# A two-layer mixer on one core: the first modulation vectors computed in quarters instead of halves, the tokens loaded in the same column pieces

## The chip, the cores and the metric

The program runs on one core of a Trainium2 chip. The metric is the device time of one execution in microseconds, and lower is better. Three runs of the kernel before are at hand; their median stands below, beside one profiled execution with its trace.

## What is computed

A two-layer transformer-like mixer works on 512 latent tokens (`x`, four tiles of 128 rows) and 256 context tokens (`ctx`, two tiles), each a vector of 1024 columns, all in float32. Each layer begins with a modulation: two conditioning vectors, one for `x` and one for `ctx`, are multiplied with `w_mod` and give six vectors of 1024 columns; the first two of them, a shift and a scale, turn the tokens into the input `h` of the in-projection:

```
mod = silu_c @ w_mod[l] + b_mod[l]
sh1, sc1, g1, sh2, sc2, g2 = [m[:, None, :] for m in jnp.split(mod, 6, axis=-1)]
...
h = x * (1.0 + sc1) + sh1
h_c = x_ctx * (1.0 + sc1c) + sh1c
proj = h @ w_in[l]
proj_c = h_c @ w_in[l]
```

The columns of `proj` go to attention, a gated MLP, pooling and a Fourier mix; an out-projection, a layer norm and a SwiGLU network with a second layer norm follow. Everything behind `proj` is the same in both kernels, apart from where a few instructions of layer 0's end stand.

## The kernel before

**Products.** Each float32 operand is split into two halves of a shorter format, the rounded value and the rest: ScalarE (ACT) casts, VectorE (DVE) subtracts (`split`, L167 to L170), and each product is three matmuls on TensorE (PE) into one accumulator (`mm3`, L172 to L175). The weights go the same way: `wload` loads a block of 832 or 1024 columns into a staging buffer, ACT casts it and DVE subtracts. There are four staging buffers and five buffers for split weights, so a cast of a new block waits until the matmuls of the block that had its buffer are through.

**Order.** The program is written as plain Python loops with generators that are advanced a step at a time (`filler`, `fill`), and a scheduler then sets the order of the instructions on each engine; an engine takes its instructions strictly in that order. Nearly all loads are issued by one queue (SP) in order. In the built program each load signals on one of eight semaphores, taken in turn, and waits for the load that had the semaphore before it to land; at the start bias loads issued by ACT hold four of the eight, and four loads of `w_mod` are in flight.

**The start.** `mods(0, (0, 1), c0, n, early=True)` computes the two vectors that layer 0's in-projection needs, for 2n columns: eight loads of `w_mod`, one per block k of 128 rows, then four small matmuls per k (L285), a bias add, transposes into columns (L312) and two copies per vector into `modT` (L315 to L319). Before the change it is called twice, for columns 0 to 511 (`ma`) and 512 to 1023 (`mb`), each with loads of 512 KB. The queue brings, in this order: `ma`'s eight loads, the first halves of four token tiles (256 KB each), the first two blocks of `w_in` (416 KB each; A0 and A2, for k = 0, 1 and k = 2, 3), the first halves of the two ctx tiles, `mb`'s eight loads, the second halves of all six tiles, then the blocks A4 and A6 of `w_in`, then blocks B1, B2 and so on (512 KB each), which the next stage multiplies with.

**The in-projection.** `inproj` goes over k = 0 to 7. For each k, `make_h` transposes the block of the six tiles on PE (L379: four for `x`, two for `ctx`), ACT applies scale and shift out of `modT` (L381), ACT casts and DVE subtracts (`u` tiles), and 18 matmuls follow: twelve for `x` into double banks (`pd`), six for `ctx` into `ps`. Blocks k = 0 to 3 need `modT` of the first half, 4 to 7 of the second. Behind `make_h` the loop advances `filler`, which holds `mb`, by two steps while k < 4 (a step is one k of `mb`). The splits of the weight blocks A4, A6, B1, B2, B3 and B4 stand on ACT and DVE between the splits of the tokens. Behind k = 7 comes the stage of the B blocks.

## Time and profile before

| | |
|---|---|
| device time, median of three runs | 1658.34 us (1655.94 to 1658.73) |
| device time of the profiled execution | 1661.08 us |
| its span, first to last instruction | 1659.3 us |
| mean granted TensorE clock | 0.984 |
| PE busy | 1573.3 us, 95% of the span |
| DVE busy | 1049.8 us, 63% |
| ACT busy | 764.9 us, 46% |
| DMA, mean over the span | 146 GB/s |

The profiled execution takes 1.78 us more than its span, and stands 2.74 us above the median. PE is busy for 95% of the span; the table alone does not tell where the rest lies, nor what the engines wait for there. The chain of work that ended last has 81% of the span on PE, 6% on DVE, 5% on DMA and 4% on ACT.

### The profile page before, as it was taken

The page shows a single profiled execution, that of the slowest core. Times are in us where ns is not written, and L with a number is a line of the kernel's source. Part 1 is how long each engine was busy: PE and PEld are TensorE (multiplying, and loading weights), DVE is VectorE, ACT ScalarE, POOL GpSimd, SP SyncE. Part 2 cuts the span into 40 slices and gives each one's busy share as a digit, 9 for nine tenths or more (in the row PEclk, how much of TensorE's full clock was granted, in tenths as well). Part 3 has the DMA queues.
Part 4 walks back from the last instruction along what each step waited for, and adds up shares of the span by engine and source line. Part 5 has one row for each costly group of instructions (what it writes and reads, how often), then busy time and mean ns, then how long its engine had stood idle before and what let it go on. Part 6 is the DMA issues. An engine that isn't in the chain of part 4 may idle for free.

```text
span 1659.3 us, 23905 instructions
## 1 busy us (share of the span) xinstructions
PE 1573.3 (95%) x9129; PEld 1361.8 (82%) x9129; DVE 1049.8 (63%) x1619; ACT 764.9 (46%) x1381; POOL 221.4 (13%) x308
## 2 busy tenths in 40 slices
PE   7998989999999999999999988989999999998997
PEld 4885668988899999997677774759988999997785
DVE  1445476876675665654457674557867888885676
ACT  2523455783653443443324543247865544553221
POOL 0232011341000000002001032422320000001003
PEclk9999999999999999999999999999999999999998
DMA  9325624118522332346965636560047344455551
GB/s 348 104 63 193 211 88 129 50 52 271 157 83 70 106 105 88 120 127 214 369 190 162 184 119 251 168 190 26 26 136 220 109 127 125 126 161 178 176 157 51
DMA packets 180503, 241.81 MB, mean 146 GB/s; under 512 B 10874, under 2 KB 127468, under 8 KB 180388
## 3 DMA queue, kind: packets, MB, share of 16 engines
q1 hardware_dynamic: 180356, 240.26, 45.3%
q8 instruction: 72, 1.18, 0.3%
q14 instruction: 43, 0.35, 0.1%
q10 hardware_dynamic: 32, 0.02, 0.0%
HBM read 215.30 MB, written 24.94 MB: 145 GB/s over the span
## 4 chain that ended last, share of the span: by engine, by line
PE 81%; DVE 6%; DMA 5%; ACT 4%; issue 2%; POOL 1%; SPq 1%; POOLq 0%; DVEq 0%; ACTq 0%
PE pd L1204 23%; PE pd L173 10%; PE pd L174 9%; PE pd L175 9%; PE ps L173 5%; PE ps L174 5%; PE ps L175 5%; PE ps L1204 4%; PE ps L747 3%; PE ps L731 2%; PE ps L285 2%; DVE w L169 2%; PE pd L285 2%; DMA u<-in_w_mod_dram 1%; ACT w L168 1%
## 5 line engine op out<-in xcount | busy, mean ns | idle before, releaser
L169 DVE TENSOR_TENSOR w<-s,w 128x1024 fp32r<-128x1024 f32 (+2 forms) x285 | 350.5, 1236 | 199.5 <-ACT w L168 198.0
L168 ACT CAST w<-s 128x1024 fp32r<-128x1024 f32 (+2 forms) x285 | 292.6, 1030 | 320.8 <-PE pd L1204 111.7
L1204 PE MATMUL pd<-u,w 128*128 128x256 f32 (+1 forms) x1938 | 297.2, 306 | 4.9 <-DVE w L169 3.1
L1204 PEld LDWEIGHTS pd<-u,w 128*128 128x128 f32 x1938 | 280.4, 189 | 10.6 <-ACT f L1258 4.5
L173 PE MATMUL pd<-w,u 128*128 128x512 f32 (+5 forms) x728 | 277.0, 381 | 7.0 <-ACT u L471 3.0
L174 PE MATMUL pd<-w,u 128*128 128x512 f32 (+5 forms) x728 | 274.3, 377 | 1.0 <-DVE w L169 1.0
L175 PE MATMUL pd<-w,u 128*128 128x512 f32 (+5 forms) x728 | 272.1, 375 | 0.0
L173 PEld LDWEIGHTS pd<-w,u 128*128 128x128 f32 x728 | 139.6, 192 | 50.4 <-issue 13.4
L174 PEld LDWEIGHTS pd<-w,u 128*128 128x128 f32 x728 | 140.0, 192 | 33.5 <-issue 10.1
L175 PEld LDWEIGHTS pd<-w,u 128*128 128x128 f32 x728 | 139.9, 192 | 29.9 <-issue 6.7
L168 ACT CAST u<-y 128x512 fp32r<-128x512 f32 (+3 forms) x186 | 94.9, 530 | 149.2 <-PE ps L175 102.8
L169 POOL TENSOR_TENSOR u<-y,u 128x512 fp32r<-128x512 f32 (+1 forms) x60 | 79.4, 1331 | 245.3 <-ACT u L168 223.9
L169 DVE TENSOR_TENSOR u<-y,u 128x512 fp32r<-128x512 f32 (+3 forms) x126 | 67.0, 551 | 70.9 <-ACT u L168 64.6
L174 PE MATMUL ps<-u,w 128*128 128x256 f32 (+2 forms) x288 | 93.0, 325 | 0.1
L175 PE MATMUL ps<-u,w 128*128 128x256 f32 (+2 forms) x288 | 92.7, 324 | 0.0
L173 PE MATMUL ps<-u,w 128*128 128x256 f32 (+2 forms) x288 | 91.9, 327 | 0.6 <-ACT f L1131 0.3
L169 DVE TENSOR_TENSOR u<-ps,u 128x512 fp32r<-128x512 f32 (+2 forms) x106 | 67.0, 655 | 35.8 <-ACT u L168 34.8
L173 PE MATMUL ps<-w,u 128*128 128x512 f32 (+1 forms) x208 | 81.2, 397 | 4.6 <-DVE u L169 4.6
L174 PE MATMUL ps<-w,u 128*128 128x512 f32 (+1 forms) x208 | 81.9, 394 | 3.5 <-DVE w L169 3.5
L175 PE MATMUL ps<-w,u 128*128 128x512 f32 (+1 forms) x208 | 81.6, 392 | 0.0
L168 ACT CAST u<-ps 128x512 fp32r<-128x512 f32 (+2 forms) x106 | 56.9, 563 | 39.3 <-PE ps L835 19.4
L1204 PE MATMUL ps<-u,w 128*128 128x384 f32 (+1 forms) x456 | 73.4, 310 | 0.0
(255 smaller groups left out, 2541.6 us busy)
## 6 DMA issues: line engine op xcount, KB each, us to landing
s<-in_w_ffn_dram SPq DMA_DIRECT2D x154, 512.0 KB
s<-in_w_out_dram SPq DMA_DIRECT2D x50, 512.0 KB
s<-in_w_mod_dram SPq DMA_DIRECT2D x48, 512.0 KB
u<-in_w_mod_dram SPq DMA_DIRECT2D x32, 512.0 KB
s<-in_w_in_dram SPq DMA_DIRECT2D x16, 512.0 KB
f<-in_w_mod_dram SPq DMA_DIRECT2D x16, 512.0 KB
yd<-f SPq DMA_DIRECT2D x19, 384.0 KB
y<-yd SPq DMA_DIRECT2D x88, 64.0 KB
```

The source lines that it names most:

```text
L168: c = A_.copy(out=hi, in_=src)
L169: (eng or V_).tensor_tensor(out=lo, in0=src, in1=f(hi), op=ALU.subtract)
L173: T_.matmul(ps, lhsT=ll, rhs=rh, start=start, stop=False)
L174: T_.matmul(ps, lhsT=lh, rhs=rl, start=False, stop=False)
L175: return T_.matmul(ps, lhsT=lh, rhs=rh, start=False, stop=stop)
L285: T_.matmul(ps[32 * j:32 * j + 32, :n], lhsT=sst[:, k, :], rhs=ws[j // 2][:, (j % 2) * n:(j % 2 + 1) * n], start=(k == 0), stop=(k == KD - ...
L731: T_.transpose(pt[:, o:o + P], es[t2][:, k * P:(k + 1) * P], ident)
L747: T_.matmul(av[:, 0:256], lhsT=vt[k][:, h, :], rhs=pts[k // 2][:, a, (k % 2) * 256:(k % 2 + 1) * 256], start=(k == 0 and a == 1), stop=(k ...
L1204: T_.matmul(ps, lhsT=A[u][:, k], rhs=B[k][:, v], start=first and k == 0 and i == 0, stop=last and k == 3 and i == 2, skip_group_check=True)
```

## The change

The first half of the modulation is computed in two quarters: `ma` for columns 0 to 255 and `mc` for 256 to 511, each with n = 128 and eight loads of 256 KB; `mb`, the second half, stays as it was. The tokens come in pieces of the same columns: 256, 256 and 512. The queue's order is now: `ma`, six token pieces of 128 KB, A0, `mc`, six pieces of 128 KB, A2, `mb`, six pieces of 256 KB, A4, A6, B1. Up to A4 it is the same bytes: 8.4 MB of `w_mod`, 3.1 MB of tokens, 0.85 MB of `w_in`, in 16 + 12 + 2 loads before and 24 + 18 + 2 after. There are twelve small bias loads on ACT's queue instead of eight. `filler` holds `mc` and `mb`; the loop advances it by five steps for k = 0 and 1 and four for k = 2 and 3, and empties `mc` ahead of k = 2. `modT` for blocks 0 and 1 now comes from `ma`, for 2 and 3 from `mc`. Two further edits touch the end of layer 0: `split` returns both its instructions, and the first part of layer 1's `make_h` (`hook`) is to be issued behind the last split of `feat`. The list `pe` and the buffers `xr_` are not read by anything.

```diff
--- before.py
+++ after.py
@@ -166,13 +166,15 @@
 
     def split(hi, lo, src, eng=None):
         c = A_.copy(out=hi, in_=src)
-        (eng or V_).tensor_tensor(out=lo, in0=src, in1=f(hi), op=ALU.subtract)
-        return c
+        return c, (eng or V_).tensor_tensor(out=lo, in0=src, in1=f(hi), op=ALU.subtract)
 
     def mm3(ps, lh, ll, rh, rl, start, stop):
         T_.matmul(ps, lhsT=ll, rhs=rh, start=start, stop=False)
         T_.matmul(ps, lhsT=lh, rhs=rl, start=False, stop=False)
-        return T_.matmul(ps, lhsT=lh, rhs=rh, start=False, stop=stop)
+        pe[0] = T_.matmul(ps, lhsT=lh, rhs=rh, start=False, stop=stop)
+        return pe[0]
+
+    pe = [None]
 
     def behind(ins, earlier):
 
@@ -210,12 +212,13 @@
     sst = cp.tile([P, KD, 32], F32, name="sst")
     gd = drp.tile([2, 2, 2, D], F32, name="gd")
     xn = drp.tile([LX, D], F32, name="xn")
+    xr_ = [drp.tile([P, D], F32, name=f"xr{i}") for i in range(NTX)]
     xc = drp.tile([LC, D], F32, name="xc")
     rd = [[drp.tile([P, D], F32, name=f"rd{l}_{i}") for i in range(NT)] for l in range(2)]
     yd = [[drp.tile([P, LJ], F32, name=f"yd{l}_{i}") for i in range(NF)] for l in range(2)]
 
 
-    bte = [cp.tile([P, 256], F32, name=f"bte{i}") for i in range(2)]
+    bte = [cp.tile([P, n], F32, name=f"bte{n}_{i}") for i, n in enumerate((256, 128, 128))]
     cr = Y(P)
     nc.sync.dma_start(out=cr[0:8], in_=g["c"].rearrange("o (k p) -> (o k) p", p=P))
     nc.sync.dma_start(out=cr[8:16], in_=g["c_ctx"].rearrange("(k p) -> k p", p=P))
@@ -449,9 +452,11 @@
                     w = getw(("A", l, gi, k), 1)
                 if l == 0:
                     extras(k)
+                    while len(filler) > 1 and k == 2:
+                        fill(1)
                 make_h(k, grp)
                 if l == 0 and k < 4:
-                    fill(2)
+                    fill(5 if k < 2 else 4)
                 if l and gi and len(filler) > 1:
                     fill(1)
                 for (st, t), a in zip(grp, acc):
@@ -1207,6 +1212,7 @@
         passes = [[(X, t) for t in range(4)]] if final else [[(C, 0), (C, 1), (X, 0)], [(X, 1), (X, 2), (X, 3)]]
 
         done = {}
+        cut = [None, None]
 
         def feat(pi, ft):
 
@@ -1230,7 +1236,8 @@
             d = U(F32R, 2 * n).rearrange("p (a b) -> p a b", a=2)
             c = split(d[:, 0], d[:, 1], y)
             if (pi, ft - 3) in done:
-                behind(c, done[(pi, ft - 3)])
+                behind(c[0], done[(pi, ft - 3)])
+            cut[:] = c
             return d, w2
 
         def unit(ft, w):
@@ -1324,7 +1331,8 @@
                     if len(filler) > 2 and (pi or ft > 1):
                         fill(1)
                     if pi and 5 <= ft < 5 + KD:
-                        hook(res, ft - 5)
+                        with tc.issue_after(cut[0].ins), tc.issue_after(cut[1].ins):
+                            hook(res, ft - 5)
                 if ft >= 8 and ft % 2 == 0 and len(ya) < len(tiles):
                     st, t = tiles[len(ya)]
                     y = FT()
@@ -1382,21 +1390,25 @@
     phase("inp")
     toks = {(st.s, t): I(n=D) for st, t in allg}
 
-    def xload(hf, grp):
+    def xload(c0, c1, grp):
         for st, t in grp:
-            nc.sync.dma_start(out=toks[(st.s, t)][:, hf * 512:(hf + 1) * 512],
-                              in_=g["x" if st.s == 0 else "ctx"][0, t * P:(t + 1) * P, hf * 512:(hf + 1) * 512])
-
-    ma = mods(0, (0, 1), 0, 256, early=True)
+            nc.sync.dma_start(out=toks[(st.s, t)][:, c0:c1],
+                              in_=g["x" if st.s == 0 else "ctx"][0, t * P:(t + 1) * P, c0:c1])
+
+    ma = mods(0, (0, 1), 0, 128, early=True)
     next(ma)
-    xload(0, allg[:4])
+    xload(0, 256, allg)
+    ahead(1)
+    mc = mods(0, (0, 1), 256, 128, early=True)
+    next(mc)
+    xload(256, 512, allg)
     ahead(2)
     mb = mods(0, (0, 1), 512, 256, early=True)
-    xload(0, allg[4:])
     next(mb)
-    xload(1, allg)
+    xload(512, 1024, allg)
     run(ma)
-    filler.append(mb)
+    filler.extend([mc, mb])
+
     one = lambda: PD()[:, 0]
     later = [mods(0, (2, 3), 0, 512, bank=one), mods(0, (4, 5), 0, 512, bank=one)]
     pars = [params(0), params(1)]
```

The scheduler gives the changed program another order. On PE, at the end of the transposes of k = 0 and the first product of the in-projection, the kernel before has (`i` are token tiles, `ps` and `pd` accumulators, `w_19` the block A0, `u_287` the split `h` of `x`):

```order
L379 MATMUL ps_288<-ident,i_171 128x128
L379 MATMUL ps_288<-ident,i_172 128x128
L379 MATMUL ps_298<-ident,i_173 128x128
L379 MATMUL ps_298<-ident,i_174 128x128
L173 MATMUL pd_283<-w_19_201,u_287 128x416
L174 MATMUL pd_283<-w_19_201,u_287 128x416
L175 MATMUL pd_283<-w_19_201,u_287 128x416
```

In the changed kernel the same place on PE reads (`u_217` to `u_231` are the eight loads of `mc`, `sst` the conditioning vectors, and `u_318` the split `h`):

```order
L382 MATMUL ps_329<-ident,i_178 128x128
L382 MATMUL ps_329<-ident,i_179 128x128
L288 MATMUL ps_336<-u_217,sst 32x128 x4
L288 MATMUL ps_336<-u_219,sst 32x128 x4
L288 MATMUL ps_336<-u_221,sst 32x128 x4
L288 MATMUL ps_336<-u_223,sst 32x128 x4
L288 MATMUL ps_336<-u_225,sst 32x128 x4
L288 MATMUL ps_336<-u_227,sst 32x128 x4
L288 MATMUL ps_336<-u_229,sst 32x128 x4
L288 MATMUL ps_336<-u_231,sst 32x128 x4
L172 MATMUL pd_314<-w_19_208,u_318 128x416
```

The 32 matmuls of the second quarter, eight rows of four, now stand between the last transposes of k = 0 and the first product. Of the 32 matmuls of `mb` (rows like the eight, with 256 columns), 24 stand ahead of the first product of k = 1 before and the last eight ahead of that of k = 2; after, sixteen stand ahead of each. All of `mb` is ahead of k = 2's products in both kernels.

On ACT, from the activation of k = 2 to the split of k = 3, the kernel before has (`y` are activated tokens with 512 columns for `x` and 256 for `ctx`; `w_52`, `w_65`, `w_80`, `w_98` are the casts of A4, A6, B1 and B2):

```order
L381 ACTIVATE y_394<-ps_391,modT 128x256
L168 CAST u_390<-y_394 128x256
L381 ACTIVATE y_430<-ps_425,modT 128x512
L168 CAST w_52_376<-s_51_375 128x832
L168 CAST u_424<-y_430 128x512
L168 CAST w_65_468<-s_64_467 128x832
L381 ACTIVATE y_437<-ps_434,modT 128x256
L168 CAST w_80_553<-s_79_552 128x1024
L168 CAST u_390<-y_437 128x256
L168 CAST w_98_660<-s_97_659 128x1024
```

The changed kernel has, from the activation of k = 2 for `x` on (`w_63`, `w_78`, `w_91` are the casts of A4, A6 and B1; `u_454` is the split of `ctx`, `u_496` that of `x` for k = 3):

```order
L384 ACTIVATE y_450<-ps_445,modT 128x512
L168 CAST u_444<-y_450 128x512
L384 ACTIVATE y_458<-ps_455,modT 128x256
L168 CAST w_63_440<-s_62_439 128x832
L168 CAST u_454<-y_458 128x256
L168 CAST w_78_549<-s_77_548 128x832
L384 ACTIVATE y_502<-ps_497,modT 128x512
L168 CAST w_91_625<-s_90_624 128x1024
L168 CAST u_496<-y_502 128x512
L384 ACTIVATE y_509<-ps_506,modT 128x256
L168 CAST u_454<-y_509 128x256
```

The cast of A4 stood behind both splits of k = 2, ahead of the split of `x` for k = 3; now it stands one split earlier, ahead of the `ctx` split of k = 2, and the casts of A6 and B1 stand ahead of the `x` split of k = 3. DVE's rows of the same splits moved alike.

Further on ACT, around k = 4 in the kernel before, the cast of B3 (`w_116`) stands so:

```order
L381 ACTIVATE y_487<-ps_482,modT 128x512
L381 ACTIVATE y_495<-ps_492,modT 128x256
L168 CAST w_116_771<-s_115_770 128x1024
L168 CAST u_481<-y_487 128x512
L168 CAST u_491<-y_495 128x256
```

In the changed kernel the cast of B3 stands behind both splits of k = 4, and the cast of B4 (`w_129`) stands as follows around k = 6:

```order
L384 ACTIVATE y_657<-ps_652,modT 128x512
L384 ACTIVATE y_665<-ps_662,modT 128x256
L168 CAST w_129_884<-s_128_883 128x1024
L168 CAST u_651<-y_657 128x512
L168 CAST u_661<-y_665 128x256
```

A cast of a weight block that waits for its buffer thus stands ahead of the two token splits of k = 4 before, and of k = 6 after. Behind that the rows of all engines are in the same order until the end of layer 0, where six small DVE operations (L368 to L370) move back by some 55 us of the program and, at the start of layer 1's in-projection, four PE instructions stand earlier.

## Rows read from the trace of the kernel before

**Rows 1.** The page: busy time of PE, and the span.

```profile
span 1659.3 us, 23905 instructions
...
PE 1573.3 (95%) x9129; PEld 1361.8 (82%) x9129; DVE 1049.8 (63%) x1619; ACT 764.9 (46%) x1381; POOL 221.4 (13%) x308
```

**Rows 2.** Stretches: length; PE, PEld, DVE, ACT, POOL busy; PEclk; DMA share; GB/s.

```profile
10.00:20.00 10.00, 7.23 (x50) 2.15 (x46) 0.79 (x5) 0.00 (x0) 0.00 (x0) 1.00 1.01 361
20.00:30.00 10.00, 7.57 (x29) 5.53 (x29) 2.99 (x4) 3.82 (x6) 0.00 (x0) 1.00 1.05 397
30.00:40.00 10.00, 10.00 (x94) 6.97 (x93) 1.81 (x3) 4.54 (x8) 0.00 (x0) 1.00 1.03 378
40.00:50.00 10.00, 8.27 (x52) 7.70 (x50) 6.21 (x12) 7.37 (x12) 0.00 (x0) 1.00 0.70 214
50.00:60.00 10.00, 8.02 (x38) 7.60 (x37) 4.22 (x7) 5.45 (x11) 0.00 (x0) 0.83 0.51 157
```

**Rows 3.** The same for a stretch of k = 4's products alone.

```profile
52.70:56.20 3.50, 3.50 (x13) 3.35 (x12) 1.14 (x3) 1.37 (x3) 0.00 (x0) 0.51 0.06 15
```

**Rows 4.** The chain of waits, in order of time: start, us, what.

```profile
3.13 7.40 DMA u<-in_w_mod_dram
10.55 6.22 DMA u<-in_w_mod_dram
16.79 6.09 DMA i<-in_ctx_dram
...
135.24 4.48 DMA s<-in_w_mod_dram
```

**Rows 5.** PE's timeline: start, us of one, then [idle before <- releaser].

```profile
16.82 1.08 PE L285 MATMUL ps<-u,sst 128*32 128x256 f32 x8 [0.88 <-DMA u<-in_w_mod_dram]
...
23.34 0.71 PE L173 MATMUL pd<-w,u 128*128 128x416 f32 x1
...
38.91 0.46 PE L173 MATMUL pd<-w,u 128*128 128x416 f32 x1
...
41.28 0.60 PE L379 MATMUL ps<-ident,i 128*128 128x128 f32 x4
...
45.20 0.46 PE L173 MATMUL pd<-w,u 128*128 128x416 f32 x1 [1.73 <-DVE u L169]
...
52.18 0.66 PE L379 MATMUL ps<-ident,i 128*128 128x128 f32 x4 [1.99 <-ACT y L381]
52.59 0.58 PE L173 MATMUL pd<-w,u 128*128 128x416 f32 x1
...
56.09 0.38 PE L174 MATMUL pd<-w,u 128*128 128x416 f32 x1
...
69.15 0.39 PE L173 MATMUL ps<-w,u 128*128 128x512 f32 x1
...
1007.15 1.92 PE L285 MATMUL ps<-f,sst 128*32 128x512 f32 x4 [2.94 <-DMA f<-in_w_mod_dram]
```

**Rows 6.** ACT's timeline: the casts of A4 and B1, a token split between.

```profile
42.60 0.88 ACT L168 CAST w<-s 128x832 fp32r<-128x832 f32 x1
43.37 0.62 ACT L168 CAST u<-y 128x512 fp32r<-128x512 f32 x1
...
45.14 1.04 ACT L168 CAST w<-s 128x1024 fp32r<-128x1024 f32 x1
...
61.45 1.05 ACT L168 CAST w<-s 128x1024 fp32r<-128x1024 f32 x1 [3.17 <-PE ps L175]
```

**Rows 7.** DVE's timeline: splits of A4, of tokens, and one of layer 1.

```profile
43.51 1.02 DVE L169 TENSOR_TENSOR w<-s,w 128x832 fp32r<-128x832 f32 x1 [2.53 <-ACT w L168]
44.45 0.69 DVE L169 TENSOR_TENSOR u<-y,u 128x512 fp32r<-128x512 f32 x1
...
47.40 0.42 DVE L169 TENSOR_TENSOR u<-y,u 128x256 fp32r<-128x256 f32 x1
47.74 1.22 DVE L169 TENSOR_TENSOR w<-s,w 128x1024 fp32r<-128x1024 f32 x1
...
902.25 1.23 DVE L169 TENSOR_TENSOR w<-s,w 128x1024 fp32r<-128x1024 f32 x1 [2.26 <-ACT w L168]
```

**Rows 8.** SP's timeline: the issue that waited for the last token piece.

```profile
39.11 0.38 SPq L192 DMA_DIRECT2D s<-in_w_in_dram  x1
```

## The prediction

> **What bounds the kernel now.** The page comes first: PE is busy for 1573.3 of 1659.3 us [rows 1], so the kernel is bound by PE, and an edit at the start is worth what it does to PE's idle or slow time there. The stretches of 10 us show where that is [rows 2]: PE does 7.23 us of work in 10 to 20 us and 7.57 in 20 to 30, all 10.00 in 30 to 40, then 8.27 and 8.02. In the first three of these the DMA engines are full (361, 397, 378 GB/s), in the next two they are not (214, 157). So the early gaps belong to loads, the later ones to something else. The chain of waits says which loads [rows 4]: two stretches of `w_mod` loads of 7.40 and 6.22 us, then a wait of 6.09 us for tokens. PE's timeline then gives the milestones [rows 5]: the first product of the in-projection at 23.34, k = 2's products from 38.91, k = 3's from 45.20 behind 1.73 us of idleness, k = 4's from 52.59 behind 1.99, the B stage from 69.15 us. k = 4's first ten products go at the lower clock: granted 0.51 [rows 3], (56.09 − 52.59)/10 = 0.35 us each, against (41.28 − 38.91)/12 = 0.20 for those of k = 2 [rows 5]; that is about 1.6 us.
>
> The wait ahead of k = 3 reads so: ACT casts A4 at 42.60 and only then the `x` split [rows 6]; DVE subtracts A4 at 43.51 for 1.02 us and only then the tokens at 44.45 [rows 7], and 45.20 follows. A weight block that k = 3 doesn't need stands ahead of a split that it does need. When A4 lands comes from the queue: the issue at 39.11 [rows 8] waited for the last token piece, A4's 0.43 MB come next, and at 378 GB/s [rows 2] take 1.1 us: 40.2. A6 follows at 41.3 and B1 (0.52 MB) at 42.7. Before, A4's landing ends no wait, since ACT comes to its cast at 42.60 only.
>
> **The change, part by part.**
>
> *Earlier first product.* Up to A4 the bytes are the same. The first product now needs the first quarter, one piece of all tokens, A0 and, as PE's order has it, the whole second quarter too: 2.10 + 0.79 + 0.43 + 2.10 = 5.41 MB. Before, 4.19 MB had landed by 16.77 us (16.79 in the chain is the step behind it) [rows 4], so 5.41 MB stand at 16.8 + 1.22/0.398 = 19.8 us; with the loads' lag (below) and the last four small matmuls some 21.5. So PE starts about 1.8 us ahead of 23.34. But this gain is not kept. All of `mb` stands ahead of k = 2's products in both programs, and its last load has the same bytes ahead of it. It lands ahead of 1.57 MB of tokens, so at 39.1 − 1.57/0.378 = 34.9 us before. After it come its four matmuls and two transposes, 0.9 us. What PE gains up front it waits off there.
>
> *The lag of the stream.* The first loads are 256 KB instead of 512, with four in flight as before. A load of 512 KB with an idle queue ahead of it took 4.48 us [rows 4]; 0.52 MB at 398 GB/s are 1.3 us of that, 3.2 do not depend on size, so an estimate for 256 KB is 3.2 + 0.7 = 3.8 us, and four in flight bring 4 x 0.262/3.8 = 276 GB/s. Before, 2.10 MB came in 6.22 us, 337 GB/s. The first quarter's 2.10 MB then take 7.6 us: a lag of up to 1.4 us. The second quarter's loads find more of the eight semaphores free, and the stream is full again. Bounds: 0, if the small loads flow like the large ones, to 2.8, if both quarters suffer. I take 1.2, a little under the estimate since tokens come in between. So `mb`'s last load lands at 36.1 and k = 2's `x` products start at about 37.1, 1.8 us ahead of 38.91; A4 lands at L = 41.4.
>
> *The weight splits, moved ahead.* This is the term that decides. k = 2's `x` products end 2.4 us after their start, at 39.5, and k = 3's transposes for `x` are done at 40.0. Then PE's next rows are k = 2's `ctx` products, whose split now stands behind A4's on ACT and DVE. It is ready at L + 0.88 (cast) + 1.02 (subtraction) + 0.42 (the tokens' own) [rows 6, 7] = 43.7. PE is idle for 3.7 us. The `x` split of k = 3 stands behind B1's in turn: B1 lands at L + 2.5, its cast takes 1.04, its subtraction 1.22 and the tokens' 0.69: L + 5.5 = 46.9. Before it was 45.20, so k = 3 is 1.7 us late. The six transposes between k = 3's products (0.6 us) are done in the wait: the end of k = 3 is 1.1 us late. So the early start of 1.8 turns into a loss, because PE's order binds it to loads that come at 41 to 44 us.
>
> *B3 and B4.* Before, k = 4's splits stood behind B3's cast: 1.99 us idle and the slow products of 1.6. After, B3's cast stands behind them, but B4's stands ahead of k = 6's splits, and it waits for the buffer that k = 5's `ctx` products release, as the cast at 61.45 waited 3.17 us for PE [rows 6]. From there to PE's next product are the cast, two token casts and a subtraction, about 2.4 us of idle time with the products that PE has left ahead, and a slow stretch again: 0.4 more than before.
>
> *Clock.* PE fell to the lower clock at 52.59 behind 1.99 us of idleness [rows 5]. An idle stretch of 3.7 us ahead of k = 2's `ctx` products may bring another: bounds 0 and 1.6; taken 0.7.
>
> *Small edits.* 32 more matmuls of 128 columns in place of 32 of 256: 1.08 us for eight of the latter [rows 5]; PE waits for loads there. Four more bias loads lie on ACT's queue in the first microseconds. The fold of six DVE operations that moves at the end of layer 0 goes to a place where DVE idles 2.26 us [rows 7], and costs nothing; without that idle time it would be 0.6 us at most. At layer 1's start four PE instructions stand earlier, two of them behind loads like the one that PE waits 2.94 us for at 1007 us [rows 5]: bounds −1.5 and +1.5, half that wait, taken 0.
>
> The sum: +1.1 + 0.4 + 0.7 = +2.2 us. Behind 69 us nothing absorbs it: PE is the bound, and the load at 135.24 is issued behind PE's own progress. The profiled execution's span goes from 1659.3 to 1661.5, its time from 1661.1 to 1663.3. It stands 2.7 us above the median; so the predicted median is 1658.34 + 2.2 = **1660.5 us**.
>
> **The rivals.**
>
> *The stream runs freely and the weights come in time.* The pieces are spread more evenly, the gap of the startup (7.40 us for the first loads [rows 4]) shrinks since the first load is half as long, and 398 GB/s hold from then. From 10.55 us to 39.1 the queue brought about 12.4 − 2.1 = 10.3 MB, 361 GB/s; at 398 GB/s that is 2.6 us less, and the shorter startup about 0.7: L = 36.9. Then the waits for A4 and B1 vanish, k = 3 starts at L + 5.5 = 42.4, 2.8 us early, its transposes' 0.6 come on top, no new slow stretch comes, and B4's 0.4 stays: −3.0 us; with the layer start's better bound −4.5. I put it between them, at 1655.0. It balances where L is near 39.5, 0.7 us earlier than before, and is over 0.2% from about 36.6 on. For it: PE had 1.73 us to win ahead of k = 3. Against it: 361 to 397 GB/s with the engines' share at 1.0 [rows 2] is a full queue already, and smaller loads don't fill it better.
>
> *The small loads starve the queue.* Lag 2.8 us, L = 43.0: k = 3 another 1.6 late, the slow stretch at its full 1.6 in place of 0.7, and half of another ahead of k = 3, 0.8: 2.2 + 1.6 + 0.9 + 0.8 = +5.5, 1663.8 us. It is slower than 0.2% from a lag of about 1.9 us. For it speaks the load of 4.48 us, against it that in 20 to 30 us the mix of 256, 416 and 512 KB went at 397 GB/s. The Trainium skill, "DMA: Bandwidth & Descriptors", section "Rules for kernel authors", asks for 1 MiB and more per load, which speaks against pieces of 128 and 256 KB. Its section on the anatomy of a DMA fits 2.0 us plus the bytes at 436 GB/s: by that 256 KB would take 2.6 us, four in flight would bring 403 GB/s, the lag would be 0 and the sum +1.0; for 512 KB it gives 3.2, and the trace has 4.48, so the trace disagrees and I don't use it.
>
> **How the numbers follow.** About 0.2% (3.3 us) is what a measurement of this kernel can tell from no change. Chances: forecast 0.52, with a range of its own from 1657.5 to 1663.5; free stream 0.26; starved 0.22. Of the forecast about a quarter lies over 1661.7, more than 0.2% above the median, and the rest within 0.2%. Faster 0.26; within 0.2% 0.40; slower 0.12 + 0.22 = 0.34. The range takes in the free case down to −5.0 (−3.5 with the layer start's −1.5) and the starved one with the layer start's +1.5: 1653.3 to 1665.3.
>
> **What the profile after would show.** Right: the first product at about 21.5 us, the eight rows of `mc` ahead of it; k = 2's `x` products at about 37; an idle stretch of 3 to 4 us ahead of its `ctx` products, ended by a DVE split behind A4; k = 3 near 47; no idle time ahead of k = 4 but some 2.4 us ahead of k = 6; the B stage near 71.3. Wrong would be: A4 landing before 39 us, or PE busy through k = 2 and 3. The step most in doubt is L, the next the clock behind the gaps.

## The result, and the profile after

The change makes the kernel slower: 1665.95 us, the median of four runs (1664.50 to 1670.71), beside 1657.14 us for the kernel before on the same chip (four runs, 1654.87 to 1658.73). The ratio is 1.0059, with a 95% interval of 1.0035 to 1.0084. A second sample of the same kernel, `changed_again` below, gave 1.0053 (1.0036 to 1.0070; six runs, median 1666.57). Two single runs that took far longer than all others (6126 us of `late_b`, 2346 us of the kernel before) are left out of the ratios. The forecast of 1660.5 was too low, and its range ended at 1665.3. The profiled execution took 1670.71 us, 9.63 us more than that of before.

The page after, to be read beside [rows 1]:

```profile
span 1668.9 us, 24072 instructions
...
PE 1577.1 (94%) x9193; PEld 1363.3 (82%) x9193; DVE 1050.2 (63%) x1624; ACT 766.6 (46%) x1381; POOL 220.6 (13%) x309
```

PE is busy for 3.8 us more and idle for 5.8 us more. The stretches at the start, with the columns of [rows 2]:

```profile
10.00:20.00 10.00, 5.77 (x55) 2.50 (x55) 2.61 (x8) 3.05 (x5) 0.00 (x0) 1.00 0.92 291
20.00:30.00 10.00, 8.38 (x65) 5.59 (x57) 1.53 (x3) 2.62 (x4) 0.00 (x0) 1.00 1.02 339
30.00:40.00 10.00, 9.35 (x93) 6.70 (x94) 1.71 (x7) 2.49 (x5) 0.00 (x0) 1.00 1.05 392
40.00:50.00 10.00, 5.77 (x28) 4.99 (x27) 4.97 (x11) 5.29 (x9) 0.00 (x0) 0.83 1.02 344
50.00:60.00 10.00, 10.00 (x60) 9.73 (x60) 4.97 (x7) 7.14 (x11) 0.00 (x0) 1.00 0.65 185
60.00:70.00 10.00, 7.91 (x37) 6.98 (x35) 3.29 (x6) 4.61 (x8) 0.00 (x0) 0.83 0.21 56
```

The queue brought 291 and 339 GB/s in the first two stretches, where it had brought 361 and 397. PE's gap now lies in 40 to 50 us: 5.77 us of work, at a mean granted clock of 0.83. The chain of waits names what stands there (start, us, what):

```profile
26.92 9.22 DMA u<-in_w_mod_dram
36.16 7.39 DMA s<-in_w_in_dram
43.58 0.89 ACT w L168
45.44 0.43 DVE u L169
45.91 0.71 PE ps L172
```

A4 lands at about 43.55 us, ACT casts it, DVE subtracts it and then the tokens, and PE's products of `ctx` for k = 2 follow. PE's timeline, beside [rows 5]:

```profile
23.32 0.72 PE L172 MATMUL pd<-w,u 128*128 128x416 f32 x1
...
39.06 0.45 PE L172 MATMUL pd<-w,u 128*128 128x416 f32 x1
...
45.91 0.71 PE L172 MATMUL ps<-w,u 128*128 128x416 f32 x1 [3.88 <-DVE u L169]
...
49.86 0.44 PE L172 MATMUL pd<-w,u 128*128 128x416 f32 x1
...
64.48 0.25 PE L240 MATMUL ps<-ident,y 41*128 41x41 f32 x1 [1.99 <-ACT y L384]
...
74.59 0.39 PE L172 MATMUL ps<-w,u 128*128 128x512 f32 x1
...
86.16 0.40 PE L172 MATMUL pd<-w,u 128*128 128x512 f32 x1
...
1049.63 0.62 PE L288 MATMUL ps<-f,sst 128*32 128x512 f32 x2
...
1081.69 0.39 PE L172 MATMUL ps<-i,u 128*128 128x256 f32 x1 [1.84 <-DVE u L169]
...
1120.31 0.48 PE L172 MATMUL ps<-ckvT,w 128*128 128x384 f32 x1
```

The same instructions of the kernel before:

```profile
81.67 0.40 PE L173 MATMUL pd<-w,u 128*128 128x512 f32 x1
...
1044.46 0.62 PE L285 MATMUL ps<-f,sst 128*32 128x512 f32 x2
...
1110.56 0.34 PE L173 MATMUL ps<-ckvT,w 128*128 128x384 f32 x1
```

The product at 81.67 stands at 86.16: the start has cost 4.5 us. At 1044.46 the distance is 5.2, and at 1110.56 it is 9.75. So in these two traces half of the loss is not at the place that was edited. To see where it arises, PE's instructions were matched between each trace and that of before, and the difference of their starts taken as the median over those within 4 us of a time of before. All kernels of this table are told below; us, positive is later than before:

| time of before, us | 103 | 200 | 345 | 776 | 980 | 1050 | 1130 | end |
|---|---|---|---|---|---|---|---|---|
| after | 4.5 | 4.4 | 0.4 | 1.0 | 5.4 | 5.2 | 9.8 | 10.0 |
| after, again | 4.5 | 4.2 | 0.0 | 0.8 | 5.1 | 4.9 | 9.5 | 9.6 |
| no_hook | 4.9 | 4.5 | 0.8 | 0.3 | 3.7 | 2.5 | 6.4 | 5.2 |
| hook_only | −1.4 | −1.1 | −2.1 | −0.5 | 1.9 | 1.9 | 2.4 | −0.2 |
| loads_only | 1.3 | 1.3 | 1.0 | 1.1 | 0.4 | 0.5 | 0.8 | 1.2 |
| tok_halves | −0.1 | −0.5 | −4.2 | −4.9 | −2.1 | −2.7 | 0.0 | 2.0 |
| cast_behind | −1.8 | −1.2 | −5.2 | −5.0 | −2.1 | −3.1 | −1.2 | −0.6 |
| cast_no_hook | 1.0 | 1.5 | −0.8 | −0.4 | −0.1 | −1.8 | 1.1 | 1.3 |
| cast_behind_act | 3.0 | 3.1 | −0.1 | 2.6 | 3.7 | 4.4 | 5.2 | 5.7 |
| cast_behind_before | −5.9 | −6.4 | −6.5 | −6.0 | −6.6 | −8.0 | −3.2 | −2.9 |
| late_b | −5.0 | −5.8 | −9.3 | −8.7 | −9.1 | −8.4 | −7.5 | −8.9 |
| late_k4 | −4.4 | −5.0 | −5.4 | −7.4 | −7.7 | −8.4 | −8.2 | −7.3 |

A row is one execution, and each is taken against the same single execution of before. That one was itself late at the start: `hook_only`, whose program is the same up to there, stands at −1.4. Single executions of one kernel lie up to some 5 us to either side of its median, so the columns tell where a difference arises, and the ratios below what it is worth.

The table gives four steps to explain: +4.5 at the start, −4.0 between 200 and 345, +4.4 between 776 and 980, +4.6 between 1050 and 1130.

### The profile page after: what moved, and what is told of

Same layout as the page of the kernel before. It is cut to its first block, busy times and chain, and to the rows that moved or that the text cites. A ratio compares the mean times of both kernels' runs of the same rounds, so it can differ in the third digit from the quotient of the medians.

```text
span 1668.9 us, 24072 instructions
## 1 busy us (share of the span) xinstructions
PE 1577.1 (94%) x9193; PEld 1363.3 (82%) x9193; DVE 1050.2 (63%) x1624; ACT 766.6 (46%) x1381; POOL 220.6 (13%) x309
## 4 chain that ended last, share of the span: by engine, by line
PE 77%; DMA 7%; DVE 6%; ACT 4%; issue 3%; POOL 1%; SPq 1%; POOLq 0%; DVEq 0%; ACTq 0%
PE pd L1209 23%; PE pd L172 9%; PE pd L173 9%; PE pd L174 9%; PE ps L172 5%; PE ps L173 5%; PE ps L174 5%; PE ps L1209 4%; PE ps L752 2%; PE ps L736 2%; DMA u<-in_w_mod_dram 2%; PE pd L288 1%; DVE w L169 1%; PE ps L288 1%; ACT w L168 1%
## 5 line engine op out<-in xcount | busy, mean ns | idle before, releaser
L172 PE MATMUL ps<-w,u 128*128 128x512 f32 (+1 forms) x208 | 82.6, 403 | 10.0 <-DVE u L169 10.0
L173 PE MATMUL ps<-w,u 128*128 128x512 f32 (+1 forms) x208 | 83.3, 400 | 3.5 <-DVE w L169 3.5
L174 PE MATMUL ps<-w,u 128*128 128x512 f32 (+1 forms) x208 | 82.8, 398 | 0.0
L168 ACT CAST u<-ps 128x512 fp32r<-128x512 f32 (+2 forms) x106 | 56.7, 564 | 40.2 <-PE ps L840 20.8
L1209 PE MATMUL pd<-u,f 128*128 128x384 f32 (+1 forms) x456 | 73.1, 309 | 0.0
```

The lines of the kernel that those rows point to most:

```text
L168: c = A_.copy(out=hi, in_=src)
L172: T_.matmul(ps, lhsT=ll, rhs=rh, start=start, stop=False)
L173: T_.matmul(ps, lhsT=lh, rhs=rl, start=False, stop=False)
L174: pe[0] = T_.matmul(ps, lhsT=lh, rhs=rh, start=False, stop=stop)
L1209: T_.matmul(ps, lhsT=A[u][:, k], rhs=B[k][:, v], start=first and k == 0 and i == 0, stop=last and k == 3 and i == 2, skip_group_check=True)
```

## The experiments

The theories, with the letters that some of the expectations use. A: the start's loss is the order of the splits, weights that come late standing ahead of token splits. Its rival E: the late stream itself sets the start, whatever the order. F: the queue is slower because SP, which issues each load, is the limit. H: behind 1050 us the loss comes from layer 1's order, which is not that of before. B: the fold of six DVE operations that the change moves at the end of layer 0 costs time.

**The fold, both ways.** `no_hook` is the changed kernel without the two waits; `hook_only` is the kernel before with them and with the edits of `split` that they need.

```diff
-                        with tc.issue_after(cut[0].ins), tc.issue_after(cut[1].ins):
-                            hook(res, ft - 5)
+                        hook(res, ft - 5)
```

> The changed kernel, but the first part of layer 1's make_h is issued as before, which puts the six small DVE operations of the fold back to their old place; the first 70 us are the changed kernel's, row by row. Theory A (the loss is made in the first 75 us, by token splits that wait behind weight blocks that land late): the fold is hidden, so the time is the changed kernel's, 1664 to 1667 us, and the B stage starts some 5 us later than in the kernel before. Theory B (half of the loss of 8.8 us is made at the end of layer 0 by the moved fold, since the trace shows the offset between the two kernels at 0.9 us near 771 us and at 5 near 920): 4 us less than the changed kernel, 1661 us.

> The kernel before with nothing but the moved fold (split returns both instructions, hook issued behind the last split). Theory A: the time of the kernel before, 1657 us within 2. Theory B: 4 us more, 1661 us, and PE's idle time between 900 and 925 us grows.

`hook_only` against before: 1.0019 (1.0007 to 1.0031; 11 runs, median 1662.05), which is +3.1 us (1.1 to 5.1), nearer to B's 4 than to A's nothing. `no_hook` against before: 1.0042 (1.0030 to 1.0055), some 2 to 3 us less than the 1.0053 and 1.0059 of the changed kernel. Each pair differs by the place of the six operations alone. In the kernel before, the cost of the fold is clear of noise. On the changed kernel it has the same sign, but the intervals overlap, and its samples are others; theory B's 1661 us, 4 us less than the changed kernel, was not reached by `no_hook`: its 1665.93 us lie in the window of theory A, by which the fold costs nothing. DVE's timeline of the changed kernel shows the operations:

```profile
896.26 2.37 DVE L371 TENSOR_TENSOR ab<-PV,modT 128x8 f32<-128x8 f32 x1
...
898.55 0.15 DVE L372 TENSOR_TENSOR ab<-PV,modT 128x8 f32<-128x8 f32 x1
...
899.00 2.36 DVE L169 TENSOR_TENSOR w<-s,w 128x1024 fp32r<-128x1024 f32 x2
```

In the kernel before, a weight split stands at this place:

```profile
895.44 4.56 DVE L169 TENSOR_TENSOR w<-s,w 128x1024 fp32r<-128x1024 f32 x2
```

The first of the six takes 2.37 us, the next of the same shape 0.15. Before, two splits took 4.56 us, where two of them take 2.36 elsewhere: the same 2.2 us. So that delay is in both kernels, and the six operations add the rest, some 0.45 us, ahead of the splits of the out-projection's weights. Behind them PE's wait for a split grows from 1.82 us before to 2.20 in `hook_only`:

```profile
907.75 0.50 PE L173 MATMUL ps<-w,u 128*128 128x512 f32 x1 [1.82 <-DVE u L169]
```

```profile
907.65 0.66 PE L172 MATMUL ps<-w,u 128*128 128x512 f32 x1 [2.20 <-DVE u L169]
```

And the clock falls. The windows of 900 to 930 us, first of before, then of `hook_only`:

```profile
900.00:930.00 30.00, 26.48 (x122) 20.98 (x121) 16.95 (x25) 16.29 (x36) 0.00 (x0) 1.00 0.67 213
```

```profile
900.00:930.00 30.00, 26.39 (x115) 20.80 (x114) 15.87 (x25) 15.59 (x33) 0.00 (x0) 0.94 0.65 212
```

The mean granted clock is 1.00 before and 0.94 behind the moved fold: PE is busy as long, for fewer instructions. `no_hook`'s clock falls there too (0.94), with the fold at its old place; another wait stands behind that, which the last part of the experiments comes to.

**The loads alone, and the tokens in halves.** `loads_only` is the kernel before with the queue of the changed one: `ma`'s blocks loaded in two quarters, tokens and weights in the new order, but one computation of the first half as before. `tok_halves` is the changed kernel with the first half of the tokens in one piece.

```diff
+            for h in range(1 if c0 else 2):
+                m = 2 * n if c0 else n
+                for k in range(KD):
+                    nc.sync.dma_start(out=wu[k].rearrange("p (t c) -> p t c", t=2)[:, :, h * m:h * m + m],
+                                      in_=src[k, :, types[0]:types[0] + 2, c0 + h * m:c0 + h * m + m])
+                yield
```

```diff
-    xload(0, 256, allg)
+    xload(0, 512, allg)
...
-    xload(256, 512, allg)
```

> The kernel before with the changed kernel's loads alone: w_mod's first half comes in 16 loads of 256 KB, the tokens in 256, 256 and 512 columns, in the changed kernel's order on the queue; the modulation is still computed in halves, with eight bias loads. The scheduler puts A4's cast behind both splits of k = 2 (one row ahead of its old place). Theory A: A4 lands 3 us later than before, near 43 to 43.6 us, as in the changed kernel, since that is the stream's doing; PE waits for it ahead of k = 3, and the time is 3 to 5 us over the kernel before, 1660 to 1662. Rival D (the stream carries the small loads as well as the large ones; the lag comes from the changed order of PE, which frees the load buffers late): A4 lands at 40 to 41, and the time is 1657 to 1658.

> The changed kernel with the tokens' first 512 columns in one piece of 256 KB per tile, all ahead of A0, in place of two pieces of 128 KB; the modulation stays in quarters. The scheduler then puts the ctx split of k = 2 ahead of A4's cast again and the x split of k = 3 ahead of B1's. Theory A: A4 lands near 42 instead of 43.6 us (twelve small loads fewer on the queue), the idle stretch of 3.9 us ahead of k = 2's ctx products is gone, the first product is late (more bytes ahead of it), and the time falls by 2 to 5 us, to 1661 to 1664. A rival C (the quarters of the modulation, not the token pieces or the splits' order, make the loss): 1665 to 1666, unchanged.

A4 lands at 43.47 us in `loads_only` and at 43.05 in `tok_halves`; the estimate for before was 40.2, and its trace has 40.19. So D, by which A4 would land at 40 to 41 us, fails: the loads by themselves make the lag, with the modulation computed in halves as before. `tok_halves` had been expected near 42. How much of the lag is due to `w_mod` in loads of 256 KB and how much to the small token pieces is not shown: the two numbers differ by less than the 1.5 us between the two traces of the changed kernel (43.56 and 45.09). But the lag costs less where A4's cast stands behind the splits of k = 2: `loads_only` is 1.3 us late at 103 us, against 4.5. The wait ahead of k = 3 that theory A expected there did not show (0.66 us). By time it is 1.0026 (1.0014 to 1.0038; 12 runs), +4.3 us; the trace shows 1.3 of that at most, and what the rest is stays open. `tok_halves` is 1.0012 (1.0001 to 1.0024; 11 runs). In it no `ctx` product of k = 2 waits for A4, and its start costs nothing (−0.1).

**The order of the splits.** `cast_behind` is the changed kernel with each pair of weight splits asked for behind the splits of k = 2, 4 and 6; the loads don't move.

```diff
-                    w = getw(("A", l, gi, k), 1)
+                    w = getw(("A", l, gi, k), 0 if l == 0 and k in (2, 4, 6) else 1)
...
+                if l == 0 and k in (2, 4, 6):
+                    with tc.issue_after(lo_[0].ins), tc.issue_after(lo_[1].ins):
+                        ahead(index[("A", l, gi, k)] + 2)
```

`cast_behind_before` is the same edit on the kernel before. `cast_behind_act` is `cast_behind` with the first twelve token pieces issued by ACT:

```diff
-    xload(0, 256, allg)
+    xload(0, 256, allg, nc.scalar)
...
-    xload(256, 512, allg)
+    xload(256, 512, allg, nc.scalar)
```

> The changed kernel, with the splits of A4, A6 and B1 to B4 held behind the token splits of their step: A4 behind both splits of k = 2, A6 behind those of k = 4, B1 to B3 behind those of k = 6. The loads keep their order. Theory A (the start's loss is the lag of the stream times the order of the splits): A4 still lands near 43.6 us, but k = 2's ctx products and k = 3 no longer wait for it; the first wait is k = 4's, at about 43.6 + 2.6 + 0.3 = 46.5 us, about when PE comes there; the B stage starts at 69 to 71 us instead of 74.6, and the time falls by 3 to 6 us, to 1660 to 1663. Rival E (the loss of the start is that of the late loads whatever the order, since k = 4 needs A4 anyway): the B stage stays at 73 to 75 us and the time at 1665 to 1666.

> The run before, and the twelve token pieces of 128 KB issued by ACT's queue instead of SP's. Theory F (SP's issue of 0.43 to 0.48 us for 131 KB, 270 to 300 GB/s, makes the lag between 11 and 17 us): SP goes on to A0 and w_mod at once, and A4 lands 1.5 to 2.5 us earlier, at 41 to 42 us. Rival G (the lag is that of small rows and small loads in the DMA engines): A4 lands at 43 to 44 as before. For the time either gives the run before's within 1.5 us, since with the splits behind the tokens A4's landing ends few waits.

> The kernel before (halves, old loads, old fold), with the splits of A6 and B1 to B4 held behind the token splits of their step. The 1.99 us of idleness ahead of k = 4 and the slow products behind it should go: the B stage starts 2 to 4 us earlier, at 65.5 to 67. With it the scheduler changes layer 1's in-projection on ACT and POOL in the same rows as the changed kernel does. Theory H (that order costs some 4 us between 1040 and 1125 us, as the traces of the changed kernel, no_hook and tok_halves show against the kernel before, hook_only and loads_only): PE waits 1.6 to 1.8 us near 1070, and the time is that of the kernel before, within 1.5 us. Rival I (that part differs by chance of the clock alone): the gain of the start stays, and the time is 2 to 4 us under the kernel before.

In `cast_behind` A4 lands as late as in the changed kernel. ACT's row of its cast:

```profile
43.47 0.88 ACT L170 CAST w<-s 128x832 fp32r<-128x832 f32 x1 [3.15 <-DMA s<-in_w_in_dram]
```

But the `ctx` products of k = 2 no longer wait for it. The start goes from +4.5 to −1.8, and the ratio to 1.0023 (1.0004 to 1.0042; 12 runs), 5 to 6 us below that of the changed kernel. A holds, and E falls: the stream is as late, and the start is 6.3 us earlier. The median of 1663.70 us is just over the 1660 to 1663 that A forecast.

`cast_behind_act` brought A0 at 14.45 us instead of 16.95, but A2 at 26.04 instead of 26.58, and A4 at 43.38. What the second issuer gained at first was lost again by 26 us, PE waits for 4.0 us for a token split at 29.36, and the time is 1.0036 (1.0019 to 1.0053). F falls, as far as this kernel can tell: a second issuer doesn't make A4 earlier.

`cast_behind_before` is 5.9 us ahead at 103 us (its B stage starts at 59.68, earlier than the 65.5 to 67 expected), and still 8.0 at 1050. By 1130 it is 3.2 ahead, and its time, 1657.79 us, can't be told from before: 0.9989 (0.9971 to 1.0006; 12 runs). It loads and computes what before does, yet loses nearly 5 us between 1050 and 1130. There its rows of layer 1's in-projection stand as in the changed kernel, not as in before.

**The other edits that leave layer 1's rows otherwise.** `late_b` is `cast_behind_before` for k = 6 alone, `late_k4` for k = 4 alone:

```diff
-                if l == 0 and k in (2, 4, 6):
+                if l == 0 and k in (6,):
```

> The kernel before, with the splits of B1 to B4 alone held behind the token splits of k = 6; A4 and A6 stay. B3 and B4 no longer stand ahead of the splits of k = 4 and k = 6, so the idle 1.99 us ahead of k = 4 goes. The scheduler gives layer 1's in-projection a third order, neither that of the kernel before nor that of the changed kernel. Theory H (layer 1's order decides whether a gain of the start is kept): the B stage 4 to 6 us earlier; with the third order cheap, 1653 to 1656 us, with it as dear as the changed kernel's, 1657 to 1659. Rival K (what the start gains is lost in the middle whatever the order): 1658 to 1660.

> The kernel before, with the splits of A6 and B1 to B3 held behind the token splits of k = 4; the same third order in layer 1 as in late_b. Theory H: the time of late_b within 1.5 us, since both clear the stall ahead of k = 4; the B stage 4 to 6 us earlier than before. Rival L (the batch of four weight splits behind k = 4 holds up k = 5's tokens on ACT and DVE): a wait of 2 us or more ahead of k = 5, and no gain.

`late_b`: 0.9972 (0.9959 to 0.9985), 1654.29 us, median of 12 runs beside 1659.39: 4.6 us faster than before, and 12 below the changed kernel on the same chip. ACT's timeline shows the four casts of B1 to B4 together, behind the splits of k = 6, and PE's the B stage at 63.01 where it was 69.15 in [rows 5]:

```profile
54.24 3.90 ACT L170 CAST w<-s 128x1024 fp32r<-128x1024 f32 x4
```

```profile
63.01 0.40 PE L175 MATMUL ps<-w,u 128*128 128x512 f32 x1
```

`late_k4` also gains 4.4 us at the start, and its trace keeps them, but its 12 runs give only 0.9991 (0.9976 to 1.0006), 2.5 us over `late_b`, where H had expected 1.5 at most. The wait of 2 us ahead of k = 5 that the rival L expected is not there either (0.80). In both, layer 1's rows are in a third order, in which PE does not wait at the place of 1081.69. PE's waits between 1060 and 1090 us (who waits <- for whom: us, times, longest), of the changed kernel:

```profile
PE ps L172 <- DVE u L169: 1.8, 1, 1.8
```

of `cast_behind_before`:

```profile
PE ps L175 <- DVE u L171: 2.9, 1, 2.9
```

and of `hook_only`, whose rows are in the order of before:

```profile
PE ps L172 <- DVE u L169: 0.2, 1, 0.2
```

Before, `loads_only` and `late_k4` have no such wait, `no_hook` one of 1.8 and `tok_halves` one of 1.6. `cast_behind` and `cast_no_hook` have the changed kernel's order too, and waits of 1.6 and 1.3. The step from 980 to 1130 us in the seven traces with that order is +4.4 in both executions of the changed kernel, 2.7 in `no_hook`, 2.1 in `tok_halves`, 3.4 in `cast_behind_before`, and only 0.9 and 1.2 in `cast_behind` and `cast_no_hook`. Without that order it is 0.5 and 0.4 in `hook_only` and `loads_only`, −0.5 in `late_k4`, 1.6 in `late_b` and 1.5 in `cast_behind_act`, so the two groups overlap. H is supported by the wait in each of these traces, but not shown: no run changes layer 1's order alone, each row is one execution, and `late_k4`, with a cheap order, is not clearly faster.

**The fold once more, and the changed kernel again.** `cast_no_hook` is `cast_behind` without the waits around `hook`; `changed_again` is the changed kernel unedited.

> cast_behind (the changed kernel with the weight splits held behind the tokens) and the fold put back to its old place; on every engine that is the only difference between the two. Theory B for the fold (it costs 2 to 3 us, since DVE comes 0.3 to 1 us later to the splits behind it, PE idles longer near 905 to 920 us and goes slow): 2 to 3 us less than cast_behind, that is 1 us over the kernel before or less, ratio 0.999 to 1.001, and in the profile no step of PE against the kernel before between 776 and 990 us. Rival M (hook_only's 3 us was chance): cast_behind's ratio, 1.002 to 1.003.

> The changed kernel once more, unedited: its loss had been taken from four runs, and its profile was of the slowest of them. Theory A and B together (start, fold and layer 1's order each cost): 1665 to 1669 us, 7 to 10 over the kernel before; in the profile the B stage again at 74 to 75 us, an idle stretch of 3 to 4.5 us ahead of k = 2's ctx products, and a wait of 1.6 to 1.9 us on PE near 1075 to 1082. Rival J (the first sample overstated it): within 4 us of the kernel before.

`cast_no_hook`: 1.0009 (0.9993 to 1.0025; 11 runs, median 1661.70), 2.3 us less than `cast_behind`; these intervals overlap, but this is the third pair with the same sign and some 2 to 3 us, and `hook_only` the one that is clear of noise. From 776 to 980 us `cast_behind` loses 2.9 us and `cast_no_hook` 0.3; their windows of 900 to 930 us repeat what `hook_only` showed:

```profile
900.00:930.00 30.00, 25.16 (x108) 19.68 (x108) 16.39 (x25) 14.33 (x31) 0.00 (x0) 0.94 0.56 173
```

```profile
900.00:930.00 30.00, 26.16 (x121) 20.71 (x120) 17.16 (x26) 16.50 (x36) 0.00 (x0) 1.00 0.63 210
```

`changed_again` comes to 1666.57 us, as A and B together expect, and not to within 4 us of before (J). It repeats the steps of the changed kernel within 0.5 us in every column of the table, the unexpected −4 at 345 us among them. Its first 70 us are not the same in detail: A4 lands at 45.09 us, 1.5 later, and the clock does not fall behind the wait ahead of k = 6 (1.00 in 60 to 70 us, where the first trace has 0.83).

**The wait near 920 us.** The step from 776 to 980 us holds more than the fold. Near 918 us PE waits a second time for a split, which needs a load of `yd`. ACT's row of the cast behind that load, first of before, then of `no_hook`:

```profile
916.44 0.51 ACT L168 CAST u<-y 128x384 fp32r<-128x384 f32 x1 [1.84 <-DMA y<-yd]
```

```profile
918.23 0.51 ACT L168 CAST u<-y 128x384 fp32r<-128x384 f32 x1 [3.42 <-DMA y<-yd]
```

The load is issued at 912.65 us before and at 912.86 in `no_hook`, and it lands at 915.9 to 916.4 and at 917.8 to 918.2. In all seven traces of kernels that compute the first vectors in quarters ACT waits for it for 2.8 to 3.4 us and PE then for 1.5 to 2.1, with the fold moved or not. In the six others it is 1.6 to 2.0 for ACT and 0.3 to 0.7 for PE. So the changed program brings this load later, which costs time in `no_hook` as well. Why it lands later was not tested.

## Why the prediction was wrong, step by step

**The lag of the stream: the step that failed at the start.** The prediction took 1.2 us with bounds of 0 and 2.8. A4 came at 43.55 instead of 40.2: a lag of 3.4, outside the bounds. It is rather more than that: the landing at 40.19 is that of the one profiled execution of before, and four other kernels with the same loads (`hook_only`, `cast_behind_before`, `late_b`, `late_k4`) have A4 at 38.2 to 38.5, while those with the new loads have it at 43.0 to 45.1. The queue's rate in windows up to A4 (columns as in [rows 2]), first before, then after:

```profile
11.00:17.00 6.00, 4.09 (x36) 0.79 (x32) 0.00 (x0) 0.00 (x0) 0.00 (x0) 1.00 0.99 338
17.00:23.00 6.00, 2.97 (x16) 1.42 (x11) 2.13 (x7) 2.85 (x4) 0.00 (x0) 1.00 1.05 400
23.00:27.00 4.00, 4.00 (x12) 3.58 (x13) 1.65 (x3) 0.97 (x2) 0.00 (x0) 1.00 1.05 394
27.00:38.00 11.00, 11.00 (x93) 7.16 (x95) 1.12 (x2) 3.64 (x6) 0.00 (x0) 1.00 1.03 381
```

```profile
11.00:17.00 6.00, 2.97 (x15) 1.46 (x15) 0.65 (x5) 1.74 (x3) 0.00 (x0) 1.00 0.87 266
17.00:23.00 6.00, 4.78 (x64) 1.64 (x64) 1.96 (x3) 1.31 (x3) 0.00 (x0) 1.00 1.08 356
23.00:27.00 4.00, 4.00 (x23) 3.58 (x16) 0.00 (x0) 0.38 (x1) 0.00 (x0) 1.00 0.97 309
27.00:38.00 11.00, 9.11 (x89) 6.64 (x92) 2.55 (x8) 3.89 (x7) 0.00 (x0) 1.00 1.04 386
```

The estimate of 276 GB/s for small loads was near the 266 of the first window. What failed is "the second quarter's loads find more of the eight semaphores free, and the stream is full again": the queue is slow through both quarters and their token pieces, 356 and 309 GB/s up to 27 us, and full only with `mb`'s loads of 512 KB. The bytes missing up to there are 6 x 72 + 6 x 44 + 4 x 85 kB = 1.04 MB, 2.7 us at 386 GB/s; some 0.6 MB are missing by 11 us already (265 GB/s before, 209 after). Two things show in these windows, and no run tells them apart by edit. From 17 to 23 us the DMA engines are as busy as before (1.08 and 1.05) and yet bring less: 2236 packets for 2.14 MB, where 1375 brought 2.40 MB. The rows of a load are half as long, and a byte took some 15% more of the engines' time. From 11 to 17 us the engines are also less busy, 0.87 instead of 0.99. The Trainium skill, "DMA: Bandwidth & Descriptors", section "Rules for kernel authors", asks for large loads, and the direction agrees with these windows. The fit that the prediction took from its section on the anatomy of a DMA and set aside is given there for loads issued by GpSimd; the loads here are issued by SP, so the 3.4 us say little about it.

**The splits behind A4: right, and its size follows from the lag.** The prediction had the `ctx` products of k = 2 at L + 2.32 and k = 3 at L + 5.5. With L = 43.55 that is 45.87 and 49.05; the trace has 45.91 and 49.86. The 0.8 us more at k = 3 go with the clock of 0.83 behind the idle time, for which the prediction had taken 0.7. PE's idleness there was forecast as 3.7 us and is 3.88. The start's loss was forecast as 2.2 us; with 2.2 us more lag it comes to 4.4, and 4.5 was found. That the two agree so closely is in part luck: in `changed_again` A4 is 1.5 us later, and the loss is again 4.5, where the slow stretch behind k = 6 is missing. The first product shows the other face of the lag: 21.5 us forecast, 23.32 found, where before had 23.34. Nothing was won that could be lost later, and k = 2's `x` products, forecast at 37, stand at 39.06. The rival of the starved queue was nearer with its lag of 2.8 us, but took less than was found, and more for the clock, and that the queue ran short of loads is only part of what the windows show, since from 17 to 23 us the engines were full.

**B4: right.** 2.4 us of idle time ahead of k = 6 were forecast, 1.99 found, as long as the one ahead of k = 4 in [rows 5], and the slow stretch behind it is in the 0.83 of 60 to 70 us, in the first of the two traces. The B stage at 74.59 is not like for like with 69.15, since four of its products stand earlier now; 86.16 against 81.67 is.

**"Behind 69 us nothing absorbs it": wrong.** Between 200 and 345 us the changed kernel wins back 4 us, in both of its executions. The win lies at two places. At the first, where the distance goes from 4.6 to 2.1 us, PE waits for a DVE result, before and after:

```profile
217.12 0.55 PE L173 MATMUL pd<-u,w 128*128 128x258 f32 x1 [2.85 <-DVE y L943]
```

```profile
220.47 0.36 PE L172 MATMUL pd<-u,w 128*128 128x258 f32 x1 [1.62 <-DVE y L948]
```

The wait is 1.2 us shorter after, and only before does the clock fall behind it (0.70 in 217 to 222 us, where the changed kernel has 1.00 from 217 to 225). Together that is the 2.5 us. At the second place, at 334 and 336 us, both kernels wait for 1.86 us, and the clock alone differs; windows before and after:

```profile
330.00:345.00 15.00, 12.45 (x71) 11.31 (x69) 12.72 (x21) 11.43 (x23) 4.92 (x6) 0.89 0.20 70
```

```profile
330.00:345.00 15.00, 12.49 (x83) 11.19 (x82) 13.93 (x24) 12.01 (x24) 5.73 (x7) 1.00 0.24 84
```

That is 1.6 us, from 2.0 to 0.4. The prediction had no term for either, and that they took 4 us off the loss was luck; other kernels win 0 to 4 us there too.

**"The fold costs nothing, and 0.6 us at most": wrong, in `hook_only` it costs 3.1 (1.1 to 5.1).** The 2.26 us of idle time of DVE in [rows 7] are there, but at 902 us, and the six operations stand at 896, ahead of splits that PE comes to wait for. Their own 0.45 us were priced about right; the drop of the clock behind the longer wait was not counted, and by the windows of `hook_only` and `cast_behind` it is what made them dear.

**"At layer 1's start four PE instructions stand earlier: bounds −1.5 and +1.5, taken 0": wrong in kind and size.** The scheduler moved more than these: the load of a `w_in` block on SP, casts on ACT and rows on POOL stand elsewhere too. The statement ahead of the prediction, that behind k = 6 the rows of all engines keep their order but for the fold and four PE rows, missed them. DVE gets to a split later, PE waits for it for 1.84 us at 1081.69, and the step from 980 to 1130 us is 0.9 to 4.4 us in the seven traces with that order. `cast_behind_before`, which has it without any change of the loads, loses 4.8 us from 1050 to 1130 alone; the old order loses about 0.5, the other two up to 1.6 from 980 on. That the order is the cause is supported and not shown.

So the sum of +2.2 lacked +2.2 for the lag, +1 to 5 for the fold, +1 to 4 for layer 1, and −4 in the middle. Together that is 2.4 to 9.4 us, where the medians and ratios of the two comparisons give 7.2 to 9.8, so the terms are too loose to be added up. Two further parts are known and not priced: the load of `yd` that lands late near 918 us, and the profiled execution of before, which was 1.4 us late at the start by `hook_only`'s trace, so that the start's loss may be nearer 5.9 than 4.5. Two slips of the prediction's arithmetic change nothing: 0.35 − 0.20 us for ten products is 1.5, not 1.6, and by its own sum the rival of the free stream balances at L = 39.9, not 39.5.

## What to carry to other kernels

Halving the size of the first loads, and with it the length of their rows, took throughput from the queue until the large loads began: price a stream by the rate of its own rows through to the last small load, not only for the first few. Where a late load feeds a cast in the middle of an in-order engine's list, the place of the cast can set the loss: with the casts of weights behind the token splits the same late stream cost nothing at the start, though the kernel as a whole stayed slower than before. On the unchanged loads the casts of B1 to B4 behind k = 6 made the one kernel here that is clearly faster than before; with all casts behind, the gain can't be told from noise. And with a scheduler in between, compare the order of every engine to the end of the program: here about half of the loss arose far from the edited place, from a small edit of its own and from rows that the scheduler moved.

## What the runs showed of the hardware that was not expected

The same idle time led to different clocks. PE's timeline before, and after, at the same instruction:

```profile
232.12 0.66 PE L731 MATMUL ps<-ident,e 128*128 128x128 f32 x4 [2.08 <-DVE u L169]
```

```profile
234.21 0.66 PE L736 MATMUL ps<-ident,e 128*128 128x128 f32 x4 [2.08 <-DVE u L169]
```

Behind 2.08 us of idleness the clock fell to its lower level (1.2 GHz; granted 0.58 on the mean of 233 to 237 us) in the kernel before, and stayed at the upper one (2.4 GHz; granted 1.00) in the changed kernel, both of its traces alike. The earlier wait, 2.85 us before and 1.62 after, does not decide it: in `loads_only` PE is idle for 2.92 us there and the clock stays up, and then it falls behind 2.09 us at the place above, while in `cast_no_hook` it falls behind 1.65 us at the earlier place and stays up behind 2.08 at the later one. In `late_b` it falls behind neither 2.29 nor 2.08 us, in `hook_only` it falls behind 1.85. So the length of an idle time between 1.6 and 2.9 us does not tell whether the clock falls. What decides is open; for a forecast it means that some microseconds of this kernel's time move with details that no row of the edited place shows.

A DVE operation of 128 x 8 elements took 2.37 us at 896.26, and the next of the same shape 0.15. Beside it POOL ran a long operation on 128 x 1024 elements:

```profile
896.00 2.61 POOL L1066 TENSOR_TENSOR f<-f,f 128x1024 f32<-128x1024 f32 x1
```

In the kernel before the weight split at 895.44 met the same delay of 2.2 us. That POOL's operation is the cause was not tested.
